# A decoder-layer kernel with a new column order, early x loads, joined RWKV output products and side work that waits for its tiling

## The chip, the cores and the metric

The kernel runs on one core of one Trainium2 chip. The metric is device microseconds (us) of one execution; lower is better. Its time before is the median of three runs.

## What is computed

One decoder layer with three token mixers beside each other (batch 1, 512 tokens, width 2048, float32), and a final norm:

```python
h = _rmsnorm(x, norm_w[l])
p = h @ w_in[l]                       # 2048 x 7824 columns
y_a = _rwkv7_mix(...)   # 16 heads of 64: generalized delta rule over 512 tokens
y_b = _moba_mix(...)    # 4 heads of 128: block-sparse causal attention
y_c = _gla_mix(...)     # 4 heads: gated linear attention with decay
mix = jnp.concatenate([y_a, y_b, y_c], axis=-1)
x = x + mix @ w_out[l]
return _rmsnorm(x, final_norm_w)
```

## The kernel before

**Projections.** Activations lie transposed: 16 tiles of 128 features by 512 tokens. Each tile of x is loaded (L1093), scaled by the norm weight into a part `hhi` (ScalarE, ACT) and a remainder `hlo` (VectorE, DVE). The division by the root mean square comes later, when a projected tile leaves its PSUM bank (`rstd_b`). A weight tile `raw` (128x512: four feature tiles of one 128-column job) is split in the same way into `hi` (ACT) and `lo` (DVE). A job of 128 columns is 16 feature tiles by three products of 128x512 (hhi·hi, hlo·hi, hhi·lo; helper `mmr`, L122), 48 in one of four PSUM banks `gb`. There are 61 such jobs and a narrow one (`low`). The string `ORDER` gives their order: `k0` is the first 128 columns of RWKV's k, `ga` its gate, `gq`, `gk`, `gv`, `gg` belong to GLA, `mq` to `mg` to MoBA. The first three jobs run interleaved, as each x tile arrives.

**Start.** ACT squares each x tile into one of three buffers, and GpSimd (POOL) adds the squares up (15 adds, L1107). `stats` then sums them over the partitions with four small products (`consts,f`), takes the inverse root on POOL (L377), and transposes the result into `rstd_b`. POOL runs in order; between its fifth and its sixth add stands the copy of `sel` (L1232) from the constants.

**Side work.** Everything else is written as Python generators (`spawn`): RWKV in four groups `q` of four heads, GLA in two, MoBA in four. They use four more PSUM banks `sb` (`bank`). A planner (`Clock`) adds up an estimated time of each engine while the program is being written; after each projection product `pump` resumes each side whose estimated inputs are there, and `force` resumes one that somebody must have. So the estimates fix the order of instructions on every engine, and nothing is decided on the chip. Products of the side work go through `mm` (L118, fp32, which the trace counts twice for each product) and `tr` (L127, transposes). Many of them use a part of the array: 128x64, 64x64, 64x128 or 32x32, against 128x128 for projections and transposes.

**RWKV.** For each pair of heads `j` in a group, `pair_r`, `pair_k`, `pair_v` form the inputs; the A stage (`AW,BK`, 64x128) makes the matrices, `solve` inverts the triangular ones on DVE (a DMA of `Ld` to DRAM and back, one multiplication by `n2l`, then some 60 short `scr` operations), and `pair_v` of `j = 1` needs `xr` (ACT and DVE, L135) for two products with `sel`. `chain` then walks eight chunks of 64 tokens; in each it makes the new state with four products `VS,BKt`. For each pair of chunks `y_pair` makes the outputs in two banks:

```python
for j in range(2):
    for h in range(2):
        ... mm(ps[h][r, j], AW[hr, c, j, 1], Sn[c % 3][hr, j], start=True, stop=False)
    for h in range(2):
        ... mm(ps[h][r, j], ARB[:, c, j, h], VS[:, c, j, h], start=(c == 0), stop=True)
```

The output projection (64 units with 12 products each) and the final norm follow when all sides are done.

Of the kernel before, what the change touches and what calls it, by code (L numbers as in the profile page):

```python
# [19 lines left out]
NC = S // C  # L20
# [19 lines left out]
ORDER = """wdad k0 ga0 ga1 r0 k1 low v0 r1 v1 gk0 gq0 gv1 gv0 gg1 gg0 k3 k2 gk1 gq1 r2  # L40
r3 v2 ga2 gv2 gg2 v3 ga3 gv3 gg3 mq0 k4 k5 r4 v4 r5 mg0 ga4 mv0 mk0 v5 k7
k6 mk1 mq1 ga5 mv1 r6 r7 v7 v6 mg1 ga6 mk2 mv2 mq2 mq3 mv3 mg2 mk3 ga7 mg3"""
# [15 lines left out]
MARGIN, BACKLOG = 0.1, 3.5  # L58
# [5 lines left out]
class Clock:  # L64


    def __init__(self):
        self.t = {"pe": 0.0, "dve": 0.0, "act": 0.0, "pool": 0.0, "dma": 0.0}
        self.cur = None
        self.table = None  # L70

# [23 lines left out]
def tile_hybrid(ctx: ExitStack, tc: tile.TileContext, x, xT, wu, wlow, wout, par, cst, w2a2_d, aup_d, fw, out):  # L95
# [19 lines left out]
    def mm(o, l, r, start=True, stop=True):  # L115
        m, n = numel(l), numel(r)
        ck.add("pe", 2 * max(m / 1.2, 2 * n / 2.4) / 1000)
        nc.tensor.matmul(o, l, r, start=start, stop=stop)  # L118

    def mmr(o, l, r, start, stop):  # L120
        ck.add("pe", numel(r) / 2400)
        nc.tensor.matmul(o, l, r, start=start, stop=stop)  # L122

    def tr(o, i):
        ck.add("pe", 0.107)
        k = i.shape[0]
        nc.tensor.transpose(o, i, ident[:k, :k])  # L127
# [50 lines left out]
    def dma(o, i, eng=None, est=3.0):  # L178
        if ck.cur is not None:
            ck.cur.ready = max(ck.cur.ready, ck.cur.start + est, ck.cur.end + est)  # L180
        (eng or nc.gpsimd).dma_start(o, i)
# [99 lines left out]
    def mixed(k, u):  # L281
# [6 lines left out]
        else:  # L288
            dma(mixd[k], u, nc.sync)
# [20 lines left out]
    def pump():  # L310

        for s in list(sides):
# [5 lines left out]
    def force(flag, what):  # L318

        while not flag():  # L320
            ready = [s for s in sides if runnable(s)]
            if not ready:
# [9 lines left out]
    def bank(n=1):  # L332
# [47 lines left out]
    def stats():  # L380
        yield lambda: squares[0] == KT
        ck.cur.start = max(ck.cur.start, ck.t["pool"])
# [7 lines left out]
        yield from rsqrt(rst[:, 4:8], rst[:, 0:4], 1.0 / D, NORM_EPS)  # L390
        b = yield from bank()
# [44 lines left out]
    def pair_decay(pr, j):  # L436
# [8 lines left out]
        b = yield from bank()  # L445
        mmr(sbk[b], w2hi[:, 0:128], wd, True, False)
        mmr(sbk[b], w2lo, wd, False, True)
        act(s0, sbk[b], AF.Sigmoid, bias=col(P_W0, pr))
        release(b)
        b = yield from bank()  # L450
        mmr(sbk[b], w2hi[:, 128:256], ad, True, False)
        mmr(sbk[b], a2lo, ad, False, True)
        act(s2, sbk[b], AF.Sigmoid, bias=col(P_A0, pr))
        release(b)
# [48 lines left out]
    def pair_v(pr, j):  # L503
# [10 lines left out]
        b = yield from bank()  # L514
# [36 lines left out]
    def bk_transposes(q):  # L551
        for c in range(0, NC, 2):
            b = yield from bank()
# [8 lines left out]
    def key_norms(q, j):  # L562
# [9 lines left out]
        dma(Nd[2 * j:2 * j + 2], n2t, nc.sync)  # L572
# [4 lines left out]
        for bl in range(2):  # L577
            for h in range(2):
                l0 = 32 * bl + 16 * h
                dma(n2l[l0:l0 + 16], Nd[h:4:2].rearrange("j (c b i) -> b j c i", b=2, c=NC)[bl], nc.sync)  # L580
# [8 lines left out]
    def solve():  # L589

        dma(Ld, Lt, nc.sync)
        yield None
        for bl in range(2):
            for h in range(2):
                r0, l0 = 64 * h + 32 * bl, 32 * bl + 16 * h
                dma(Lm[l0:l0 + 16], Ld[r0:r0 + 32, :, :, 32 * bl:32 * bl + 32].rearrange("i j c t -> (j c) i t"),
                    nc.sync)
# [15 lines left out]
        dma(Xd, NR[0:32], nc.sync)  # L613
        dma(Td, Lm, nc.sync)
        yield None
        for h in range(2):
            dma(T11[64 * h:64 * h + 32], Xd[16 * h:16 * h + 16].rearrange("l t s -> t l s"), nc.sync)
        for bl in (1, 0):
            for h in range(2):
                r0, l0 = 64 * h + 32 * bl, 32 * bl + 16 * h  # L620
                dma(Ttf[r0:r0 + 32, :, 32 * bl:32 * bl + 32], Td[l0:l0 + 16].rearrange("l s t -> s l t"), nc.sync)
# [24 lines left out]
    def y_pair(q, cp):  # L646

        bs = yield from bank(2)
# [11 lines left out]
        flags[f"ymm{q}"] = cp + 1  # L660
        yield None
        yo = Yq[:, cp].rearrange("p (r h n) -> p r h n", r=2, h=2)
# [8 lines left out]
    def chain(q):  # L671
# [3 lines left out]
        for c in range(NC):  # L675
# [21 lines left out]
            yield None  # L697
            if c < NC - 1:
                b = yield from bank()
# [18 lines left out]
            if c % 2:  # L718
                spawn(f"y{q} {c // 2}", y_pair(q, c // 2))
# [3 lines left out]
    def group_norm(q):  # L723
# [14 lines left out]
        for j in range(2):  # L738
            pr = 2 * q + j
            b = yield from bank()  # L740
# [33 lines left out]
    def load_w2a2(pr):  # L774
        dma(w2a2, w2a2_d[:, 256 * pr:256 * pr + 256], nc.sync)
# [24 lines left out]
    def by_chunks(src, parts):  # L800

        b = yield from bank()
# [12 lines left out]
    def gla(g):  # L815
# [14 lines left out]
        dma(aup, aup_d[:, 128 * g:128 * g + 128], nc.sync)  # L830
        if g == 0:
            yield from evac("low", lowT, rows=32)
            dma(lowd, lowT, nc.sync)
        else:
            dma(lowT, lowd, nc.sync)
# [31 lines left out]
        b = yield from bank()  # L867
# [23 lines left out]
        for w in range(4):  # L891
            b = yield from bank()
# [5 lines left out]
            for e in range(2):  # L898
# [6 lines left out]
                if e == 0:  # L905
                    yield None
                    bo = yield from bank(2)
# [22 lines left out]
        for i in range(2):  # L930
# [3 lines left out]
            b = yield from bank()  # L934
# [9 lines left out]
    def moba(h):  # L944
# [5 lines left out]
        def window(w, p, pT):  # L950
# [3 lines left out]
            b = yield from bank()  # L954
# [13 lines left out]
            b = yield from bank()  # L968
# [5 lines left out]
            b = yield from bank()  # L974
# [14 lines left out]
        b = yield from bank()  # L989
# [64 lines left out]
    loaded, split_done = 0, 0  # L1054
    late_adds, squares_of = [], []
# [41 lines left out]
    def square(n, r):  # L1097
# [6 lines left out]
        while late_adds and (len(late_adds) > 2 or n == KT - 1):  # L1104
            m, e = late_adds.pop(0)
            ck.add("pool", 1.25, e + 0.2)
# [33 lines left out]
    def split(i):  # L1140
        kind, n = items[i]
        dep = load_end[i]
        if kind == "x":
# [3 lines left out]
                               dep=max(dep, ck.t["act"] + 0.2))  # L1147
            squares_of.append((n, r))
# [251 lines left out]
```

## Time and profile before

| | |
|---|---|
| median of 3 runs | 1059.04 us (1058.44 to 1060.01) |
| the profiled execution | 1058.42 us, of which the span of its instructions 1056.7 us |
| mean granted TensorE clock | 0.995 of full speed |
| TensorE (PE) busy | 1035.9 us, 98% of the span |
| DVE, ACT, POOL busy | 666.3, 442.9, 71.9 us (63%, 42%, 7%) |
| DMA | 111.35 MB, 104 GB/s of HBM over the span |

The share of busy time says which engine has the least slack; the waits say where it stood still, and the chain of work that ended last is followed back from the last instruction to what released each step. A line number in a row is the line of the helper, so tiles (`gb`, `sb`, `VS`, `xr`) tell which step it is; `sb<-Sn,AW` is the product of `Sn` and `AW` into a side bank.

### The profile page before, as it was taken

What the parts mean: (1) busy time and instruction counts of PE and PEld (TensorE: products, weight loads), DVE (VectorE), ACT (ScalarE), POOL (GpSimd) and SP (SyncE); (2) the same over time, 40 slices, a digit from 0 to 9 for tenths busy, and PEclk for the clock granted to TensorE, in tenths of its full rate; (3) what the DMA queues carried; (4) which work ended last, traced back from release to release, by engine and by line L of the source; (5) the groups of instructions that cost most, each with busy time, mean ns of one, the idle gap of its engine ahead of it and who ended that gap; (6) DMA issues with size and microseconds to landing.
All of it is one profiled execution on the core that took longest, in us unless ns stands there. A gap on an engine that the chain in (4) does not pass through costs nothing.

```text
span 1056.7 us, 16747 instructions
## 1 busy us (share of the span) xinstructions
PE 1035.9 (98%) x6376; PEld 819.5 (78%) x6376; DVE 666.3 (63%) x1346; ACT 442.9 (42%) x789; POOL 71.9 (7%) x73
## 2 busy tenths in 40 slices
PE   7799999999999999999999999999999999999996
PEld 6587888767788887778888777888877788888885
DVE  6646759656756785676788665666965665424343
ACT  6464543343464433235434423545322365323333
POOL 4500000000100000001000001000000010202020
PEclk9899999999999999999999999999999999999999
DMA  7332333422233342223334222333341265343534
GB/s 253 100 93 78 92 92 98 111 56 84 81 108 88 98 115 74 71 81 114 92 99 119 67 71 70 90 99 86 115 111 51 71 223 175 109 142 100 160 119 159
DMA packets 80112, 111.35 MB, mean 105 GB/s; under 512 B 28176, under 2 KB 29392, under 8 KB 79904
## 3 DMA queue, kind: packets, MB, share of 16 engines
q1 hardware_dynamic: 79888, 109.23, 35.4%
q8 instruction: 50, 0.82, 0.3%
q0 software_dynamic: 144, 1.05, 0.2%
q14 instruction: 30, 0.25, 0.1%
HBM read 98.36 MB, written 11.89 MB: 104 GB/s over the span
## 4 chain that ended last, share of the span: by engine, by line
PE 97%; ACT 1%; POOL 1%; issue 0%; DMA 0%; DVE 0%; SPq 0%; ACTq 0%; POOLq 0%
PE gb L122 74%; PE sb L118 11%; PE sb L122 9%; PE sb L127 2%; POOL f L1107 1%; DMA raw<-in_wu_dram 0%; ACT hhi L175 0%; ACT hi L175 0%; DVE lo L135 0%; ACT f L175 0%; ACT pbuf L175 0%; ACT ARB L175 0%; DVE VS L135 0%; ACTq L1396 0%; POOLq L1396 0%
## 5 line engine op out<-in xcount | busy, mean ns | idle before, releaser
L122 PE MATMUL gb<-hhi,hi 128*128 128x512 f32 x976 | 404.1, 414 | 5.8 <-ACT hi L175 5.8
L122 PE MATMUL gb<-hhi,lo 128*128 128x512 f32 x976 | 383.5, 393 | 0.5 <-DVE lo L135 0.5
L122 PE MATMUL gb<-hlo,hi 128*128 128x512 f32 x976 | 382.9, 392 | 0.0
L175 ACT ACTIVATE hi<-raw 128x512 fp32r<-128x512 f32 x296 | 186.1, 630 | 394.5 <-PE gb L122 290.9
L135 DVE TENSOR_TENSOR lo<-raw,hi 128x512 fp32r<-128x512 f32 x296 | 212.7, 722 | 216.7 <-ACT hi L175 209.9
L122 PEld LDWEIGHTS gb<-hhi,hi 128*128 128x128 f32 x976 | 184.3, 189 | 49.6 <-ACT hi L175 6.0
L122 PEld LDWEIGHTS gb<-hhi,lo 128*128 128x128 f32 x976 | 184.1, 189 | 41.4 <-DVE lo L135 1.1
L122 PEld LDWEIGHTS gb<-hlo,hi 128*128 128x128 f32 x976 | 184.7, 189 | 34.2 <-DVE hlo L141 1.0
L135 DVE TENSOR_TENSOR scr<-scr 64x30 f32<-64x30 f32 (+14 forms) x240 | 77.5, 323 | 7.1
L122 PE MATMUL gb<-hi,hhi 128*128 128x512 f32 x128 | 50.0, 391 | 0.0
L122 PE MATMUL gb<-hi,hlo 128*128 128x512 f32 x128 | 49.8, 389 | 0.0
L122 PE MATMUL gb<-lo,hhi 128*128 128x512 f32 x128 | 49.8, 389 | 0.0
L175 ACT ACT_TABLE_LOAD x34 | 43.6, 1283 | 1.0 <-DVE VS L155 0.4
L155 DVE COPY VS<-sb 64x128 f32<-64x128 f32 x64 | 18.5, 288 | 32.8 <-PE sb L118 31.7
L377 POOL TENSOR_TENSOR gn<-gn,mhalf 128x16 f32<-128x16 f32 (+1 forms) x5 | 13.0, 2602 | 309.0 <-DVE gn L151 309.0
L175 ACT ACTIVATE Lt<-sb 64x256 f32<-64x256 f32 (+1 forms) x64 | 19.3, 326 | 33.1 <-PE sb L118 30.5
L175 ACT ACTIVATE f<-sb 64x256 f32<-64x256 f32 (+3 forms) x52 | 17.3, 363 | 36.1 <-PE sb L127 19.6
L122 PE MATMUL sb<-lo,hhi 128*128 128x512 f32 x80 | 31.2, 390 | 0.0
L122 PE MATMUL sb<-hi,hhi 128*128 128x512 f32 x80 | 31.2, 389 | 0.0
L122 PE MATMUL sb<-hi,hlo 128*128 128x512 f32 x80 | 31.2, 389 | 0.0
L122 PE MATMUL sb<-late,hhi 128*128 128x512 f32 x96 | 30.2, 395 | 0.0
L122 PEld LDWEIGHTS gb<-lo,hhi 128*128 128x128 f32 x128 | 24.0, 188 | 5.0
(230 smaller groups left out, 1140.5 us busy)
## 6 DMA issues: line engine op xcount, KB each, us to landing
raw<-in_wu_dram SPq DMA_DIRECT2D x244, 256.0 KB
raw<-in_wout_dram SPq DMA_DIRECT2D x64, 256.0 KB
f<-in_x_dram SPq DMA_DIRECT2D x16, 256.0 KB
hlo<-mix SPq DMA_DIRECT2D x15, 256.0 KB
Ld<-Lt SPq DMA_DIRECT2D x4, 512.0 KB
mix<-ARB SPq DMA_DIRECT2D x8, 256.0 KB
mix<-f SPq DMA_DIRECT2D x7, 256.0 KB
AW<-in_xT_dram SPq DMA_DIRECT2D x6, 256.0 KB
```

The costliest lines, as they stand in the source:

```text
L118: nc.tensor.matmul(o, l, r, start=start, stop=stop)
L122: nc.tensor.matmul(o, l, r, start=start, stop=stop)
L127: nc.tensor.transpose(o, i, ident[:k, :k])
L135: nc.vector.tensor_tensor(o, a, b, op=op)
L155: nc.vector.tensor_copy(o, a)
L175: nc.scalar.activation(o, a, f, **kw)
L377: nc.gpsimd.tensor_tensor(r, v, mhalf[:, 0:n], op=ALU.pow)
L1107: nc.gpsimd.tensor_tensor(fb[0], fb[0], fb[1 + m % 3], op=ALU.add)
```

## The change

Six things change. (1) `ORDER` is another permutation of the same jobs. (2) The planner's estimates are others: products of one tiling are cheaper and a change of tiling costs extra, an add on POOL costs 1.63 instead of 1.25, DMAs queue behind each other, and `pump` goes twice over the sides. (3) `bank` takes the tiling of the products to come, and waits up to 4 planned us (`PATIENCE`) until the engine is in it, unless the step is forced. (4) The products of `y_pair` are in `y_products`; where three banks are free at an odd chunk, they directly follow the `VS,BKt` products of that chunk, all `VS,ARB` first and all `Sn,AW` behind. (5) The loads of x tiles 4 to 15 are issued before weight loads that have to wait for a buffer. (6) The copy of `sel` stands behind the inverse root. The helper `dma` issues on SP alone.

```diff
+        old, self.tiling = self.tiling, tiling
+        if old != tiling:
+            whole = (old in "rf") + (tiling in "rf")
+            cost += 0.1 + 0.1 * (whole == 1) - 0.1 * (old == "r" and tiling == "f")
+        return self.add("pe", cost)
...
-        for s in list(sides):
+        for s in 2 * list(sides):
...
-    def bank(n=1):
+    def bank(n=1, tiling=None, patience=PATIENCE):
+
+        if tiling is not None and ck.tiling != tiling:
+            limit = ck.t["pe"] + patience
+            yield lambda: ck.tiling == tiling or forcing[0] or ck.t["pe"] > limit
...
-        ck.cur.start = max(ck.cur.start, ck.t["pool"])
+        ck.cur.start = max(ck.cur.start, ck.t["pool"] + 2.0)
...
         yield from rsqrt(rst[:, 4:8], rst[:, 0:4], 1.0 / D, NORM_EPS)
+        ck.add("pool", 0.3)
+        nc.gpsimd.tensor_copy(sel, consts[:, K_BD:K_BD + 130])
...
+    def y_products(q, cp, bs):
+
         ps = [sbk[b][:, 0:128].rearrange("p (r n) -> p r n", r=2) for b in bs]
         cs = [(2 * cp, slice(0, 64)), (2 * cp + 1, slice(64, 128))]
+        for j in range(2):
+            for h in range(2):
+                for c, r in cs:
+
+                    mm(ps[h][r, j], ARB[:, c, j, h], VS[:, c, j, h], start=(j == 0), stop=(c == 0), skip=True)
         for j in range(2):
             for h in range(2):
                 hr = slice(64 * h, 64 * h + 64)
                 for c, r in cs:
                     if c:
-                        mm(ps[h][r, j], AW[hr, c, j, 1], Sn[c % 3][hr, j], start=True, stop=False)
-            for h in range(2):
-                for c, r in cs:
-                    mm(ps[h][r, j], ARB[:, c, j, h], VS[:, c, j, h], start=(c == 0), stop=True)
+                        mm(ps[h][r, j], AW[hr, c, j, 1], Sn[c % 3][hr, j], start=False, stop=True, skip=True)
...
+            yb = None
             if c < NC - 1:
-                b = yield from bank()
+                if c % 2 and len(free_banks) >= 3:
+                    b, *yb = yield from bank(3)
+                else:
+                    b = yield from bank()
...
                         mm(pw[r, j], BKt[:, c, j, r], VS[:, c, j, h])
+                if yb is not None:
+                    y_products(q, c // 2, yb)
...
+    x_items = [i for i, (kind, n) in enumerate(items) if kind == "x" and n >= 4]
+    rest = [i for i in range(len(items)) if i not in x_items]
+    load_order = rest[:7]
+    for i, ahead in zip(rest[7:], (1, 3, 2, 3, 3)):
+        load_order += x_items[:ahead] + [i]
+        x_items = x_items[ahead:]
...
-            nc.gpsimd.tensor_copy(sel, consts[:, K_BD:K_BD + 130])
```

Three places of the order of instructions. First PE, in the RWKV output of the first two chunks of group 0 (`Sn_131` is the state after chunk 0). Before:

```order
L122 MATMUL gb_161<-hhi_87,lo_107 128x512
L118 MATMUL sb_168<-Sn_131,AW 64x64
L118 MATMUL sb_165<-Sn_131,AW 64x64
L118 MATMUL sb_168<-VS,ARB 64x64 x2
L118 MATMUL sb_165<-VS,ARB 64x64 x2
L118 MATMUL sb_168<-Sn_131,AW 64x64
L118 MATMUL sb_165<-Sn_131,AW 64x64
L118 MATMUL sb_168<-VS,ARB 64x64 x2
L118 MATMUL sb_165<-VS,ARB 64x64 x2
L122 MATMUL gb_161<-hhi_89,hi_100 128x512
```

And after:

```order
L133 MATMUL gb_161<-hhi_67,lo_105 128x512
L129 MATMUL sb_167<-VS,BKt 64x64 x4
L129 MATMUL sb_166<-VS,ARB 64x64 x2
L129 MATMUL sb_165<-VS,ARB 64x64 x2
L129 MATMUL sb_166<-VS,ARB 64x64 x2
L129 MATMUL sb_165<-VS,ARB 64x64 x2
L129 MATMUL sb_166<-Sn_131,AW 64x64
L129 MATMUL sb_165<-Sn_131,AW 64x64
L129 MATMUL sb_166<-Sn_131,AW 64x64
L129 MATMUL sb_165<-Sn_131,AW 64x64
L133 MATMUL gb_161<-hhi_69,hi_101 128x512
```

Four groups that alternate between two tilings (`Sn,AW` uses 64 rows of the array, `VS,ARB` and `VS,BKt` 128, all 64 columns) have become one of twelve products and one of the `Sn` products, in the same stay as the state products. Before, those stood by themselves 17 rows ahead.

Second DVE, around the first use of the statistics (`gn` from `sb_165` is their sum, the TENSOR_SCALAR on `gn` precedes POOL's inverse root, `lo` are weight remainders). Before:

```order
L141 SCALAR_TENSOR_TENSOR hlo_96<-sgt_147,params,hhi_95 128x512
L135 TENSOR_TENSOR lo_106<-raw_98,hi_102 128x512
L135 TENSOR_TENSOR lo_107<-raw_99,hi_103 128x512
L155 COPY gn<-sb_165 128x4
L135 TENSOR_TENSOR lo_104<-raw_97,hi_100 128x512
L151 TENSOR_SCALAR gn<-gn 128x4
```

And after:

```order
L152 SCALAR_TENSOR_TENSOR hlo_96<-sgt_147,params,hhi_95 128x512
L146 TENSOR_TENSOR lo_106<-raw_98,hi_102 128x512
L146 TENSOR_TENSOR lo_107<-raw_99,hi_103 128x512
L146 TENSOR_TENSOR lo_104<-raw_97,hi_100 128x512
L166 COPY gn<-sb_165 128x4
L146 TENSOR_TENSOR lo_105<-raw_98,hi_101 128x512
L162 TENSOR_SCALAR gn<-gn 128x4
```

The statistics stand one weight tile later on DVE, in front of the scaling is now `lo_105`. On PE their small products moved from behind projection product 108 to behind product 120, and the transposes of the result from behind 120 to behind 132.

Third DVE, from the solve of group 0 to `xr` of its second pair (the `scr` rows are steps of the solve). Before:

```order
L135 TENSOR_TENSOR lo_104<-raw_97,hi_100 128x512
L135 TENSOR_TENSOR f_152<-gb_164,rstd_b 128x512
L141 SCALAR_TENSOR_TENSOR vT<-pbuf_138,params,vT 128x512
L135 TENSOR_TENSOR lo_105<-raw_98,hi_101 128x512
L135 TENSOR_TENSOR scr<-scr 64x198
...
L135 TENSOR_TENSOR scr<-scr 64x12x19
L141 SCALAR_TENSOR_TENSOR f_152<-f_152,f_149 128x512
L135 TENSOR_TENSOR lo_106<-raw_99,hi_102 128x512
L135 TENSOR_TENSOR xr_122<-s_144,xr_121 128x512
```

And after:

```order
L146 TENSOR_TENSOR lo_107<-raw_99,hi_103 128x512
L152 SCALAR_TENSOR_TENSOR vT<-pbuf_138,params,vT 128x512
L146 TENSOR_TENSOR scr<-scr 64x198
...
L146 TENSOR_TENSOR scr<-scr 64x12x19
L146 TENSOR_TENSOR lo_104<-raw_97,hi_100 128x512
L146 TENSOR_TENSOR xr_122<-s_144,xr_121 128x512
```

Two operations on `f_152` (the evacuation of a gate and its product) and two weight remainders have gone from this stretch of DVE. On PE, the projection products between the last A-stage product of a group and the product that needs this `xr` were 99, 153, 204 and 102 in groups 0 to 3; they are 75, 150, 105 and 195.

## Rows read from the trace of the kernel before

**Rows 1.** Waits of PE: who waited for whom, us in total, times, longest.

```profile
PE sb L118 <- POOL f L1107: 6.0, 1, 6.0
```

**Rows 2.** A stretch: length, busy us (instructions) of PE, PEld, DVE, ACT, POOL, PE clock, DMA share, GB/s.

```profile
27.00:48.00 21.00, 14.56 (x57) 11.12 (x57) 14.89 (x15) 9.51 (x17) 14.93 (x13) 0.84 0.30 93
```

**Rows 3.** The chain that ended last, in order of time: start us, us, what.

```profile
42.20 4.53 PE gb L122 x12
...
144.35 1.99 PE sb L118 x32
...
344.21 1.09 PE sb L118 x16
...
355.08 27.93 PE gb L122 x123
```

**Rows 4.** Timeline of PE: start us, us, engine, line, operation, tiles, form, count.

```profile
215.25 0.40 PE L122 MATMUL gb<-hhi,lo 128*128 128x512 f32 x1
215.58 0.45 PE L118 MATMUL sb<-VS,BKt 128*64 128x64 f32 x8
215.96 0.50 PE L122 MATMUL gb<-hhi,hi 128*128 128x512 f32 x1
216.30 0.40 PE L122 MATMUL gb<-hlo,hi 128*128 128x512 f32 x1
```

**Rows 5.** Timeline of PE, in a `y_pair`.

```profile
244.29 0.34 PE L118 MATMUL sb<-Sn,AW 64*64 64x64 f32 x8
244.56 0.45 PE L118 MATMUL sb<-VS,ARB 128*64 128x64 f32 x8
```

**Rows 6.** Timeline of PE, transposes of an A stage.

```profile
148.45 0.60 PE L127 MATMUL sb<-consts,BK 128*128 128x128 f32 x4
148.81 0.71 PE L122 MATMUL sb<-xr,sel 128*128 128x512 f32 x2
```

**Rows 7.** Timeline of PE, the products of the statistics and the transposes of the result.

```profile
40.34 1.86 PE L118 MATMUL sb<-consts,f 128*128 128x1 f32 x8 [5.98 <-POOL f L1107]
...
46.57 0.60 PE L127 MATMUL sb<-consts,gn 128*128 128x128 f32 x4
```

**Rows 8.** Timeline of POOL at the start, with the idle time before a row and its releaser.

```profile
8.06 8.19 POOL L1107 TENSOR_TENSOR f<-f,f 128x512 f32<-128x512 f32 x5 [6.15 <-ACT f L175]
23.73 0.29 POOL L1232 CAST sel<-consts 128x130 fp32r<-128x130 f32 x1 [7.49 <-DMA consts<-in_cst_dram]
...
43.17 1.03 POOL L377 TENSOR_TENSOR gn<-gn,mhalf 128x4 f32<-128x4 f32 x1 [2.89 <-DVE gn L151]
```

**Rows 9.** Timeline of DVE at the start.

```profile
15.01 1.78 DVE L135 TENSOR_TENSOR lo<-raw,hi 128x512 fp32r<-128x512 f32 x1
16.71 0.74 DVE L141 SCALAR_TENSOR_TENSOR hlo<-AW,params,hhi 128x512 fp32r<-128x512 f32 x1
17.38 1.40 DVE L141 SCALAR_TENSOR_TENSOR hlo<-BK,params,hhi 128x512 fp32r<-128x512 f32 x2
```

**Rows 10.** Groups of POOL's instructions: line, operation, count | busy us, mean ns | idle before.

```profile
L1309 POOL TENSOR_TENSOR VS<-VS,AW 128x512 f32<-128x512 f32 x3 | 3.9, 1300 | 0.0
```

**Rows 11.** Timeline of SP: a weight load when its buffer came free.

```profile
34.18 0.33 SPq L1093 DMA_DIRECT2D raw<-in_wu_dram  x1
```

**Rows 12.** Timeline of ACT: the split that waited for that load.

```profile
36.77 0.63 ACT L175 ACTIVATE hi<-raw 128x512 fp32r<-128x512 f32 x1 [0.31 <-DMA raw<-in_wu_dram]
```

**Rows 13.** Timeline of PE, group 0: the products with that `xr`.

```profile
170.68 0.62 PE L122 MATMUL sb<-xr,sel 128*128 128x512 f32 x2
```

**Rows 14.** Timeline of DVE, group 0: first operation of the solve, and `xr`.

```profile
155.30 1.22 DVE L135 TENSOR_TENSOR scr<-scr,n2l 64x1024 f32<-64x1024 f32 x1 [3.14 <-DMA scr<-Ld]
...
169.69 0.68 DVE L135 TENSOR_TENSOR xr<-s,xr 128x512 fp32r<-128x512 f32 x1
```

**Rows 15.** Timeline of DVE, group 1: `xr`, and eight steps of the solve.

```profile
381.77 0.68 DVE L135 TENSOR_TENSOR xr<-s,xr 128x512 fp32r<-128x512 f32 x1
...
383.58 2.42 DVE L135 TENSOR_TENSOR scr<-scr 64x150 f32<-64x150 f32 x8
```

More of the change, by code (lines that the diff above doesn't have):

```diff
@@ L70, in __init__, with pe @@
         self.table = None
+        self.tiling = "r"
+    def pe(self, cost, tiling):
+        old, self.tiling = self.tiling, tiling
[3 more added lines that the diff above has]
+        return self.add("pe", cost)
     def add(self, eng, cost, dep=0.0):
@@ L112, in numel, with mm @@
         return n
-    def mm(o, l, r, start=True, stop=True):
+    def mm(o, l, r, start=True, stop=True, skip=False):
         m, n = numel(l), numel(r)
-        ck.add("pe", 2 * max(m / 1.2, 2 * n / 2.4) / 1000)
-        nc.tensor.matmul(o, l, r, start=start, stop=stop)
+        rows, cols = (min(q for q in (32, 64, 128) if q >= v) for v in (l.shape[0], m))
+        if rows == cols == 128:
+            ck.pe(2 * max(0.105, n / 1200 + 0.0025), "f")
+        else:
+            ck.pe(2 * (n / 2400 + 0.0025), f"{rows}x{cols}")
+        nc.tensor.matmul(o, l, r, start=start, stop=stop, skip_group_check=skip)
     def mmr(o, l, r, start, stop):
-        ck.add("pe", numel(r) / 2400)
+        ck.pe(numel(r) / 2400 + 0.0135, "r")
         nc.tensor.matmul(o, l, r, start=start, stop=stop)
     def tr(o, i):
-        ck.add("pe", 0.107)
+        ck.pe(0.0925, "f")
         k = i.shape[0]
@@ L513, in pair_v @@
         yield None
-        b = yield from bank()
+        b = yield from bank(1, "f")
         for w in range(4):
@@ L552, in bk_transposes @@
         for c in range(0, NC, 2):
-            b = yield from bank()
+            b = yield from bank(1, "f")
             for i in range(4):
@@ L655, in y_pair @@
                     if c:
-                        mm(ps[h][r, j], AW[hr, c, j, 1], Sn[c % 3][hr, j], start=True, stop=False)
-            for h in range(2):
-                for c, r in cs:
-                    mm(ps[h][r, j], ARB[:, c, j, h], VS[:, c, j, h], start=(c == 0), stop=True)
+                        mm(ps[h][r, j], AW[hr, c, j, 1], Sn[c % 3][hr, j], start=False, stop=True, skip=True)
         flags[f"ymm{q}"] = cp + 1
+    def y_pair(q, cp, bs=None):
+        if bs is None:
+            bs = yield from bank(2)
+            y_products(q, cp, bs)
         yield None
+        ps = [sbk[b][:, 0:128].rearrange("p (r n) -> p r n", r=2) for b in bs]
         yo = Yq[:, cp].rearrange("p (r h n) -> p r h n", r=2, h=2)
@@ L739, in group_norm @@
             pr = 2 * q + j
-            b = yield from bank()
+            b = yield from bank(1, "f")
             for cp in range(4):
@@ L800, in by_chunks @@
     def by_chunks(src, parts):
-        b = yield from bank()
+        b = yield from bank(1, "f")
         for w in range(4):
@@ L891, in gla @@
         for w in range(4):
-            b = yield from bank()
+            b = yield from bank(1, "64x64")
             for e in range(2):
@@ L933, in gla @@
             yield flag(f"gg{h}")
-            b = yield from bank()
+            b = yield from bank(1, "f")
             for w in range(4):
@@ L967, in window @@
             yield None
-            b = yield from bank()
+            b = yield from bank(1, "f")
             for i in range(w + 1):
@@ L973, in window @@
             yield flag(f"mv{h}")
-            b = yield from bank()
+            b = yield from bank(1, "f")
             for i in range(w + 1):
@@ L988, in moba @@
         yield from evac(f"mv{h}", fb[2])
-        b = yield from bank()
+        b = yield from bank(1, "f")
         for w in range(4):
@@ L1054, in tile_hybrid @@
     loaded, split_done = 0, 0
+    x_items = [i for i, (kind, n) in enumerate(items) if kind == "x" and n >= 4]
[4 more added lines that the diff above has]
+        x_items = x_items[ahead:]
+    load_order += rest[len(load_order) - 12 + len(x_items):]
+    assert not x_items and sorted(load_order) == list(range(len(items)))
     late_adds, squares_of = [], []
@@ L1167, in advance @@
         while split_done <= last:
-            while loaded < len(items) and (slot_of.get(loaded, 0) < NRAW
-                                           or last_in_slot[slot_of.get(loaded, 0) - NRAW] < split_done):
-                load(loaded)
+            while loaded < len(items):
+                i = load_order[loaded]
+                if slot_of.get(i, 0) >= NRAW and last_in_slot[slot_of[i] - NRAW] >= split_done:
+                    break
+                load(i)
                 loaded += 1
```

68 lines of the change are left out of this document (34 added, 34 removed).

## The prediction

> **What bounds the kernel now.** The waits of PE come first. The longest, 6.0 us for POOL [rows 1], lies at the start; after 48 us there is none. The busy time by stretches shows the same: from 27 to 48 us PE works for 14.56 of 21 us, at a granted clock of 0.84 [rows 2]. The chain of work that ended last is the same list: it runs on PE nearly alone, in stretches like 123 products in 27.93 us, or 0.227 each [rows 3]. So PE sets the time, and three things can be gained or lost: PE time itself, the start, and new waits where there were none. About 861 of the 1,036 busy us are 3,792 such products, which the change keeps.
>
> **PE time: groups of small products.** The timeline shows what a group costs. The last projection product before it starts 0.33 us ahead of it instead of 0.23, four products (eight in the trace) take 0.38, and the first projection product behind it takes 0.34 [rows 4]. So entering costs 0.10 more and returning 0.11. What of the 0.38 is fixed follows from the A stage: 16 products (32 in the trace) of 128 columns take 1.99 and eight take 1.09 [rows 3], so eight more cost 0.90, 0.11 each or 0.056 for 64 columns, and 0.19 of the group is fixed. The 0.38 is then four times 0.056 and 0.15 fixed. In `y_pair`, four `Sn,AW` take 0.27 up to the `VS,ARB` behind them [rows 5]; those have the shape of `VS,BKt`, and 0.38.
>
> I counted the groups in the order of both kernels. Those with tiling 128x64 go from 88 to 61, with 64x64 from 77 to 63, together 41 fewer by 0.15: -6.15. Those with 64x128 go from 10 to 12, by 0.19: +0.4. Entries from projections go from 122 to 124 (+0.2), returns to them from 121 to 113 (-0.9). Steps straight from transposes into a tiling go from 8 to 1; I take 0.09 for each, as an entry: -0.6. The sum is **-7.1 us**. A check by the pair: before, four groups (0.27 + 0.38, twice) and 0.21 for the excursion make 1.51. Joined, eight `VS,ARB` at 0.056 and eight `Sn,AW`, for which I take 0.27 + 4 x 0.056 = 0.49, add 0.94 to a stay that the state products had anyway: -0.57, eleven times; the five others save less. That this is most of 7.1 fits. The bounds: -4.5, if the `Sn` products keep the pace of a short group and the merged groups of GLA give nothing; -8, if each removed change also gives back an entry.
>
> The waiting for a tiling (`PATIENCE`) also gathers transposes: full-array groups go from 87 to 61. I cost this at nothing. Four transposes take 0.36 us from the start of the first to the next product [rows 6], 0.09 each, and the projection product before them starts the usual 0.23 ahead, so an excursion to them has no price to save. Bounds: -1 to +0.5, since each extra tiled neighbour could cost one entry of 0.1.
>
> **The start.** Before, the statistics stop PE: their products begin at 40.34 after 5.98 us of idleness [rows 7], because POOL did only five adds by 16.25 and then stood 7.49 us for the constants that the copy of `sel` needs [rows 8]. The low clock costs as well: behind the wait twelve products take 4.53 us [rows 3] where 2.72 is usual, and the eight small ones 1.73 (40.34 to 42.07, where the next begins). So product 120 is done at 46.57, where the transposes begin [rows 7].
>
> In the changed order POOL runs on without `sel`, and the x tiles are asked for earlier. Then DVE sets the pace: a two-input operation of 128x512 takes a step of 1.70 us beside a POOL add (15.01 to 16.71) and 0.67 without (16.71 to 17.38) [rows 9]. From 8.3 us on DVE has 24 such operations ahead of the last x tile's products, 15 beside adds and 9 not: 15 x 1.70 + 9 x 0.67 = 31.5, so at 39.8. Product 120 follows about three units' products later, some 0.7 us, at 40.5, with PE in short pauses but never for six us. That is 6.1 us earlier. A part is lost again. The scaling of the statistics on DVE now stands behind `lo_105`, whose weight load goes out when `lo_106` frees its buffer at about 40.5. Such a load was issued at 34.18 [rows 11], and ACT had it at 36.77 [rows 12]: 2.6. With the split on ACT (0.63), on DVE (0.67), the scaling (0.16) and POOL's 1.03 [rows 8] the inverse root is there at 45.6. PE is at its transposes at 40.5 + 0.44 (four small products) + 12 x 0.227 = 43.7, and waits 1.9; I take 2.6 with the semaphore steps between five engines. So the start gives 6.1 - 2.6 = **-3.5 us**. Bounds: -7 without that wait and with x tiles that let POOL's fifteen adds end at 33; +2 if x arrives as late as before and the new wait comes on top.
>
> A rule speaks against this gain. The rows show a pair of one add and one DVE operation in 1.70 us; apart, an add takes 1.30 [rows 10] and the operation 0.67. So they overlap by 0.27. The Trainium skill (SBUF — State Buffer, "Who interferes with whom") says that a DVE instruction with two SBUF inputs and a GpSimd instruction that reads SBUF contend for a shared port pair, and that the second to issue is blocked for the whole of the first. That the two slow each other this trace shows; a full exclusion it does not, as 1.70 is under 1.97. By the rule fifteen pairs would take 4.1 us more, and the start would give +0.6 instead of -3.5.
>
> **New waits.** The new order of columns pulls work closer together. In group 0 the products with `xr` of the second pair stand 24.3 us behind the end of the A stage (144.35 + 1.99, then 170.68) [rows 3, 13], and DVE had `xr` at 169.69 + 0.68 = 170.37 [rows 14], 0.3 ahead: DVE, which begins the solve at 155.30 when `Ld` has come back by DMA and then runs without a pause, is on the edge already. After, DVE has four operations like `xr` fewer in the stretch, 0.68 each by that row and about 0.6 as they overlap, so 24.0 - 2.4 = 21.6 us. PE has 75 projection products instead of 99 and 16 transposes, 17.0 + 1.5, with four `sel` products and entries 0.8: 19.3. It will wait **2.3 us**. In group 1 `xr` came 37.2 us after the A stage (345.3, that is 344.21 + 1.09, to 381.77 + 0.68) [rows 3, 15]. The change puts eight more steps of the solve ahead of it (2.35 [rows 15]), two evacuations (0.7) and two operations fewer (-1.2): 39.0 us. PE has 150 x 0.227 + 20 x 0.09 + 0.8 = 36.6: **2.4 us**. In group 2 I get 26.4 against 26.6, in group 3 45.4 against 46.6: no wait. Together **+4.8**. Bounds: 0, if the trip of `Ld` through DRAM is 2.4 us shorter, to +9, if groups 2 and 3 and the group norms wait as well.
>
> **The sum.** -7.1 - 3.5 + 4.8 = -5.8. The profiled execution took 1058.42 us (1056.7 of span and 1.7 around it), so 1052.6; the median lies 0.62 above that execution, so **1053.2 us**.
>
> **Rivals.** *The waits do not come* (chance 0.12): DVE gets `xr` in time since its operations move with it. Then -10.6, 1048.4. For it speaks that the planner reckons with the same operations; against it, that in both groups the reckoning is with measured stretches.
> *The gains are small* (0.08): -4.5 in PE time, nothing at the start because x comes too late, +4.8 in waits: 1059.3, no change. That the change does not do what it says, in that waiting for a tiling gathers only transposes, belongs here.
> *Adds and DVE operations exclude each other* (0.04): where fifteen adds run back to back, each pair takes 1.30 + 0.67. Then -7.1 + 0.6 + 4.8 = -1.7, 1057.3. The pairs of before took 1.70, which leaves it little. This is the rule of the page cited above.
> *Slower: the clock at the start* (0.06). Before, products behind the long wait ran at a lower clock: twelve in 4.53 us, 0.38 each [rows 3]. A start that DVE paces has many short pauses of PE; if these hold it at the lower of its two levels, 1.2 GHz, products take twice 0.227 from 27 to 45 us, and 18 us of such work are worth 9 us less the pauses, 8.5. It decides from about 8 us on, where it eats the gain: -5.8 + 8.5 = +2.7, 1061.7. Against it: PE had stood 5.98 us at once before it was slow [rows 7], and no pause of the new start is near that.
>
> **How the numbers follow.** The forecast has 0.70. About 0.2%, or 2.1 us, is what a measurement of this kernel can tell from no change. The forecast's own bounds reach a bit into that, the first rival lies beyond: faster 0.80, same 0.14, slower 0.06. The range from 1047.5 to 1057.5 takes in the forecast with its bounds and most of the first rival, and leaves out most of the others.
>
> **What would show it.** Right: no wait of PE for the adds of POOL, product 120 near 40.5 us, a wait of 2 to 3 us before the transposes of the statistics; PE waits for DVE `xr` twice, near 163 and 378 us; groups of twelve products `VS,BKt` and `VS,ARB` of about 0.84 us; PE busy 7 us less. Wrong: idle PE after 48 us of over 8 us, a clock under 0.9 from 27 to 45 us, or PE busy unchanged.

## The result

The changed kernel takes **1054.49 us** (median of 5 runs, 1052.84 to 1055.10) against 1059.04 (1058.44 to 1060.01): a ratio of 0.9949, 95% interval 0.9937 to 0.9962. Forecast were 1053.2 and a range of 1047.5 to 1057.5. The profiled execution took 1054.49 us, of which the span is 1052.6, 4.1 less than before.

The page of the changed kernel, its span and busy time (PE is 6.3 us less busy than in the table of before; busy time counts slow products too, before the change at the start and here behind a wait told of below, so 6.3 is not yet the work saved):

```profile
span 1052.6 us, 16723 instructions
PE 1029.6 (98%) x6376; PEld 814.9 (77%) x6376; DVE 669.7 (64%) x1346; ACT 441.9 (42%) x790; POOL 74.8 (7%) x73
```

The waits of PE in the changed kernel (who waited for whom: us in total, times, longest):

```profile
PE gb L133 <- ACT hi L186: 5.8, 1, 5.8
PE sb L133 <- DVE xr L146: 4.0, 2, 2.4
PE gb L133 <- DVE hlo L152: 1.8, 4, 0.7
PE sb L138 <- POOL gn L398: 1.4, 1, 1.4
PE sb L138 <- DVE Lt L146: 0.9, 1, 0.9
```

The 6.0 us for POOL's adds [rows 1] are gone. In their place stand four short pauses for `hlo`, 1.4 us for the statistics, and, where there was no wait, 4.0 us for `xr` and 0.9 for `Lt`.

**The start.** POOL in the changed kernel, with idle time and releaser in brackets; it answers to [rows 8]:

```profile
8.07 11.58 POOL L1150 TENSOR_TENSOR f<-f,f 128x512 f32<-128x512 f32 x7 [6.16 <-ACT f L186]
21.55 6.76 POOL L1150 TENSOR_TENSOR f<-f,f 128x512 f32<-128x512 f32 x4 [1.91 <-ACT f L186]
29.49 5.20 POOL L1150 TENSOR_TENSOR f<-f,f 128x512 f32<-128x512 f32 x3 [1.17 <-ACT f L186]
35.78 1.28 POOL L1150 TENSOR_TENSOR f<-f,f 128x512 f32<-128x512 f32 x1 [1.09 <-ACT f L186]
43.13 1.03 POOL L398 TENSOR_TENSOR gn<-gn,mhalf 128x4 f32<-128x4 f32 x1 [6.06 <-DVE gn L162]
```

The adds end at 37.06 instead of 40.3, and PE at the statistics, to be held beside [rows 7], has 120 projection products done when it comes to them and 132 at the transposes:

```profile
37.67 0.50 PE L133 MATMUL gb<-hlo,hi 128*128 128x512 f32 x1 [0.25 <-DVE hlo L152]
...
38.95 0.95 PE L129 MATMUL sb<-consts,f 128*128 128x1 f32 x8
...
44.22 0.65 PE L138 MATMUL sb<-consts,gn 128*128 128x128 f32 x4 [1.45 <-POOL gn L398]
44.62 0.48 PE L133 MATMUL gb<-hhi,hi 128*128 128x512 f32 x1
```

Before, the transposes at 46.57 had 120 products ahead of them. Twelve more at 0.227 would have been 2.7 us later, at about 49.3; the changed kernel is there at 44.2, so it leads by 5.1 us.

**PE work.** A joined group in the changed kernel (timeline of PE; the count is twice that of the program):

```profile
222.22 0.45 PE L129 MATMUL sb<-VS,BKt 128*64 128x64 f32 x8
222.50 0.64 PE L129 MATMUL sb<-VS,ARB 128*64 128x64 f32 x16
223.07 0.46 PE L129 MATMUL sb<-Sn,AW 64*64 64x64 f32 x16
223.46 0.50 PE L133 MATMUL gb<-hhi,hi 128*128 128x512 f32 x1
```

Twelve products take 0.85 us up to the `Sn` group, and the eight `Sn,AW` 0.39.

**What came back.** The stretches around the second wait for `xr` (columns as in [rows 2]), and the chain behind it:

```profile
376.00:379.00 3.00, 0.61 (x3) 0.20 (x2) 2.76 (x10) 0.63 (x1) 0.00 (x0) 0.98 0.43 132
379.00:382.00 3.00, 3.00 (x8) 2.33 (x9) 2.76 (x8) 0.29 (x1) 0.64 (x2) 0.50 0.31 87
382.00:385.00 3.00, 3.00 (x14) 2.41 (x13) 2.51 (x4) 0.49 (x2) 0.00 (x0) 0.95 0.17 54
```

```profile
378.07 0.69 DVE xr L146
...
379.54 8.90 PE gb L133 x33
```

PE stood 2.39 us, and then the granted clock was at the lower of its two levels, 1.2 GHz: 33 products took 8.90 us instead of 33 x 0.227 = 7.49. That wait cost 2.4 and 1.4.

So the difference of 4.1 us divides as follows: 5.1 gained until the statistics are done; 5.1 lost in waits behind 48 us (4.0 and 0.9 of the list, and 0.2 for `VS`); 1.4 in slow products behind one of them; and what remains, 4.1 - 5.1 + 5.1 + 1.4 = 5.5, is less PE work. Counted directly it is 5.5 too: PE's busy time from the 150th projection product to the end (columns as in [rows 2]) is 994.48 us before and 990.38 in the changed kernel, of which 1.4 are the slow products.

```profile
53.64:1060.00 1006.36, 994.48 (x6216) 786.86 (x6214) 630.40 (x1305) 411.74 (x737) 44.65 (x43) 1.00 0.35 101
48.59:1060.00 1011.41, 990.38 (x6216) 784.92 (x6214) 631.09 (x1306) 412.07 (x739) 47.08 (x43) 0.99 0.34 101
```

### The profile page after: what moved, and what is told of

It reads as the page before. It is cut to its first block, busy times and chain, and to the rows that moved or that the text cites. A ratio compares the mean times of both kernels' runs of the same rounds, so it can differ in the third digit from the quotient of the medians.

```text
span 1052.6 us, 16723 instructions
## 1 busy us (share of the span) xinstructions
PE 1029.6 (98%) x6376; PEld 814.9 (77%) x6376; DVE 669.7 (64%) x1346; ACT 441.9 (42%) x790; POOL 74.8 (7%) x73
## 4 chain that ended last, share of the span: by engine, by line
PE 89%; DVE 5%; issue 2%; DMA 2%; ACT 1%; SPq 0%; POOL 0%; ACTq 0%; POOLq 0%; DVEq 0%
PE gb L133 67%; PE sb L129 10%; PE sb L133 9%; PE sb L138 2%; DVE scr L146 2%; DVE lo L146 2%; DMA raw<-in_wu_dram 1%; DVE hlo L152 1%; DMA scr<-Ld 0%; DMA Ld<-Lt 0%; DMA AW<-in_xT_dram 0%; ACT hhi L186 0%; DVE gn L170 0%; DVE Lt L146 0%; ACT hi L186 0%
## 5 line engine op out<-in xcount | busy, mean ns | idle before, releaser
L133 PE MATMUL gb<-hhi,hi 128*128 128x512 f32 x976 | 399.9, 410 | 5.8 <-ACT hi L186 5.8
```

## The experiments

Each median stands beside runs of the kernel before on the same chip, whose median was 1059.02 to 1059.44 throughout. Two kernels whose intervals overlap are not told apart by their medians; what is said of them then rests on the traces, each of which is one execution.

| kernel | median us | ratio to before (95%) |
|---|---|---|
| before + copy of `sel` moved | 1055.42 | 0.9968 (0.9956 to 0.9980) |
| before + x ahead | 1058.23 | 0.9994 (0.9985 to 1.0002) |
| before + both | 1053.20 | 0.9945 (0.9933 to 0.9958) |
| changed, `sel` back | 1056.22 | 0.9976 (0.9967 to 0.9985) |
| changed, statistics' scaling behind their copy | 1052.52 | 0.9943 (0.9930 to 0.9955) |
| changed, `xr` early | 1051.68 | 0.9937 (0.9925 to 0.9950) |
| changed, these two repairs | 1052.14 | 0.9934 (0.9922 to 0.9946) |
| changed, alternating groups | 1060.98 | 1.0018 (1.0009 to 1.0028) |
| changed, no waiting for a tiling | 1059.58 | 1.0004 (0.9995 to 1.0013) |
| changed, old column order | 1072.09 | 1.0130 (1.0114 to 1.0146) |
| before + both + grouped `y_pair` | **1049.67** | 0.9910 (0.9897 to 0.9924) |
| changed, once more | 1053.62 | 0.9946 (0.9934 to 0.9959) |

### The start: which of its parts

Only the copy moved, in the kernel before:

```diff
         yield from rsqrt(rst[:, 4:8], rst[:, 0:4], 1.0 / D, NORM_EPS)
+        nc.gpsimd.tensor_copy(sel, consts[:, K_BD:K_BD + 130])
...
-            nc.gpsimd.tensor_copy(sel, consts[:, K_BD:K_BD + 130])
```

> The kernel before with one line moved: the copy of sel stands behind the inverse root on POOL instead of between its fifth and sixth add. Loads, column order and PE order stay as before. Theory A (the copy in POOL's queue is what stopped PE for 6 us): the wait of PE for the adds shrinks to under 2 us, the clock stays up from 27 to 48 us, and the time falls by 4 to 6 us, to 1053 to 1055. Rival (late x tiles hold the adds in any case): the wait stays at 5 us or more and the time is within 1 us of 1059.

It took 1055.42 us, just outside theory A's figure, and the wait shrank as it said. The waits, and the stretch of [rows 2] in that kernel:

```profile
PE sb L118 <- POOL f L1108: 1.9, 1, 1.9
```

```profile
27.00:48.00 21.00, 18.79 (x74) 14.90 (x73) 16.07 (x18) 8.24 (x14) 11.27 (x12) 0.84 0.41 128
```

In one point theory A was wrong: PE is 4.2 us busier in this stretch than in [rows 2], but the clock is at 0.84 still, behind a wait of 1.9 us. The profiled execution was also the slowest of six (1057.65, mean clock 0.995); the two with a mean clock of 0.998 took 1053.63 and 1054.08. So the copy in POOL's queue was what held PE; but the low clock of before did not need six idle us.

Only the loads, by the change's `load_order`, in the kernel before:

> The kernel before with the x tiles 4 to 15 loaded ahead of blocked weight loads, sel still copied between the adds. Theory A: POOL still stands until the constants have landed, at 23 to 25 us, and does ten adds after it, so PE waits 4 us or more for them and the time stays within 2 us of 1059. Rival (late x): the adds end by 36 us, and the time falls by 4 us or more.

1058.23 us, and PE waited 3.7 us for the adds, a little under what theory A asked; they end at 40.98, since POOL stands for the constants as before. The loads alone are worth some 0.8 us, which the interval does not tell from nothing.

Both together:

> The kernel before with both changes of the start that leave PE's order alone: sel copied behind the inverse root, and the x tiles loaded ahead. The statistics keep their place behind projection product 108. If the two add up, 3.6 and 0.8 us, the time is 1054 to 1055. If the later place of the statistics on PE (behind product 120) is what pays once the adds are early, this gives no more than the moved copy alone, 1055 to 1056, with 1.5 to 2 us of waits at the statistics.

1053.20 us, 5.9 less than its before, where 3.6 and 0.8 add up to 4.4; the intervals are too wide to call that more than the sum. The same stretch, and PE and DVE at the statistics:

```profile
27.00:48.00 21.00, 19.58 (x90) 15.53 (x90) 16.84 (x18) 10.19 (x18) 11.53 (x12) 1.00 0.34 102
```

```profile
37.66 0.95 PE L118 MATMUL sb<-consts,f 128*128 128x1 f32 x8
...
41.62 0.65 PE L127 MATMUL sb<-consts,gn 128*128 128x128 f32 x4 [0.81 <-POOL gn L377]
```

```profile
40.10 0.15 DVE L155 COPY gn<-sb 128x4 f32<-128x4 f32 x1
40.28 0.17 DVE L151 TENSOR_SCALAR gn<-gn 128x4 f32<-128x4 f32 x1
```

With both, PE has 90 matmuls in the stretch against 74, and the clock stays up. But the loads did not leave the order alone, though the expectation says so. By the count in the trace the planner put the statistics behind product 114 and the transposes behind 123, and on DVE the scaling came directly behind the copy; the kernel with the loads alone has the same two places on PE. Behind product 108, done at 35.4, the statistics would have waited about 1.1 us for the adds, which end at 36.49 here (an estimate from the trace). So whether their later place is needed for the gain has not been separated. The main finding does not hang on it: **these two edits alone are as fast as the whole change**, 1053.20 us against 1054.49 and 1053.62, with overlapping intervals.

The copy put back into the changed kernel:

> The changed kernel with the copy of sel back at its old place, all else as changed (statistics behind projection product 120, x tiles ahead). If the moved copy by itself carries the gain at the start, POOL's adds end near 40 us again and the time rises by 4 to 5 us, to 1058 to 1059. If the later place of the statistics on PE carries it, PE has twelve products to do in that time, waits about 1 us more at most, and the time stays within 1.5 us of 1054.5.

1056.22 us, 1.7 more, and PE waited only 0.4 us for the adds: by the time this lies near the second case. By the start it lies nearer the first. POOL's ten adds behind the copy, PE at the transposes, and the stretch of [rows 2] in that kernel:

```profile
24.94 16.36 POOL L1148 TENSOR_TENSOR f<-f,f 128x512 f32<-128x512 f32 x10
```

```profile
47.17 0.65 PE L138 MATMUL sb<-consts,gn 128*128 128x128 f32 x4 [0.32 <-POOL gn L398]
```

```profile
27.00:48.00 21.00, 17.47 (x68) 12.07 (x67) 15.83 (x16) 10.96 (x19) 15.54 (x13) 0.92 0.29 87
```

The adds end at 41.30, and the transposes stand at 47.17 instead of 44.22: the copy costs 2.95 us of the 5.1 that the start had gained. Some 2 us of them come back later, because here the second wait for `xr` is 1.8 us and no slow products follow it. So the later place of the statistics keeps about 2.1 us of the gain, and the place of `sel` gives the rest.

The scaling directly behind the copy of the statistics, in the changed kernel:

```diff
         vcopy(rst[:, 4:8], sbk[b][:, 0:4])
         release(b)
-        yield None
         yield from rsqrt(rst[:, 4:8], rst[:, 0:4], 1.0 / D, NORM_EPS)
```

> The changed kernel with one pause of the planner taken out, so that on DVE the scaling of the statistics follows directly on their copy instead of behind a weight remainder that waits for its load. Theory (the 1.4 us wait before the transposes of the statistics is DVE's order): the wait goes, and the time falls by 1.5 to 2 us, to 1052.5 to 1053. Rival (POOL or the planner's other work delays it as much): the wait stays at 1 us or more and the time within 0.7 us of 1054.5.

1052.52 us, 2.0 less by the median, with overlapping intervals. The trace shows that no wait is left at the transposes, which now begin at 42.37 behind product 129: 1.2 us earlier than in the changed kernel when the three products are allowed for. DVE in that kernel:

```profile
40.38 0.16 DVE L166 COPY gn<-sb 128x4 f32<-128x4 f32 x1
40.58 0.17 DVE L162 TENSOR_SCALAR gn<-gn 128x4 f32<-128x4 f32 x1
42.49 0.69 DVE L146 TENSOR_TENSOR lo<-raw,hi 128x512 fp32r<-128x512 f32 x1 [1.75 <-ACT hi L186]
```

In the changed kernel the scaling had stood behind such a `lo`, at 42.89. The theory holds for the wait and its cause; that it is worth 1.5 to 2 us is more than the trace shows.

### The PE work: groups of small products

Every instruction at its place, only the products within a `y` in the order of before (the lines that tell the planner the old sum are left out):

```diff
         for j in range(2):
             for h in range(2):
-                for c, r in cs:
-                    mm(ps[h][r, j], ARB[:, c, j, h], VS[:, c, j, h], start=(j == 0), stop=(c == 0), skip=True)
...
-        for j in range(2):
-            for h in range(2):
                 hr = slice(64 * h, 64 * h + 64)
                 for c, r in cs:
                     if c:
-                        mm(ps[h][r, j], AW[hr, c, j, 1], Sn[c % 3][hr, j], start=False, stop=True, skip=True)
+                        nc.tensor.matmul(ps[h][r, j], AW[hr, c, j, 1], Sn[c % 3][hr, j], start=True, stop=False)
+            for h in range(2):
+                for c, r in cs:
+                    nc.tensor.matmul(ps[h][r, j], ARB[:, c, j, h], VS[:, c, j, h], start=(c == 0), stop=True)
```

> The changed kernel with every instruction at its place, but within each stay of the RWKV output the Sn and ARB products alternate between the two tilings as before (Sn, ARB, Sn, ARB). 44 more groups of 128x64 and 64x64. Theory (each group has a fixed cost of 0.15 us on PE): PE busy rises by 5 to 7 us, waits stay as they are, and the time rises to 1060 to 1061. Rival (the fixed part is hidden in the weight loads once groups follow each other directly): within 1.5 us of 1054.5.

```profile
PE 1035.4 (98%) x6376; PEld 818.2 (77%) x6376; DVE 669.8 (63%) x1346; ACT 442.5 (42%) x790; POOL 75.0 (7%) x73
```

1060.98 us, and PE 5.8 us busier: 0.13 for each of the 44 groups. But the wait for `xr` was shorter here (3.1 in all, longest 1.7) and the clock did not fall, so the changed kernel's 1.4 us of slow products hide a part. Without them, and without the start, the price comes out clearer. PE from the 150th projection product to the end (columns as in [rows 2]), in the changed kernel once more, whose clock did not fall either (its run is told of further below), and in this one:

```profile
49.45:1060.00 1010.55, 988.70 (x6216) 783.82 (x6214) 630.96 (x1306) 411.71 (x739) 47.09 (x43) 1.00 0.35 101
48.69:1060.00 1011.31, 995.42 (x6216) 787.54 (x6214) 631.14 (x1306) 412.38 (x739) 47.14 (x43) 1.00 0.34 101
```

That is 6.7 us more, or 0.15 for each group, 27 of 128x64 and 17 of 64x64. The theory holds. This grouping is the whole of the change's PE gain: with these groups back, PE works no shorter than in the kernel before (994.48 us in the same stretch).

No waiting for a tiling (the test in `bank` replaced by `if False`):

> The changed kernel with bank never waiting for a tiling; the planner then places some side work otherwise, with 81 full-array groups instead of 61 and 65 of 64x64 instead of 63. Theory (an excursion to transposes has no fixed price): PE busy without its waits rises by no more than 1 us, and what the time changes beyond that is in waits that the trace lists. Rival (each gathered excursion saves 0.2 us): PE busy without waits rises by 4 us, to a time of 1058 to 1059.

```profile
PE 1031.8 (98%) x6376; PEld 814.6 (77%) x6376; DVE 668.6 (63%) x1346; ACT 435.4 (41%) x785; POOL 74.7 (7%) x73
```

```profile
PE sb L133 <- DVE xr L146: 5.3, 4, 2.5
```

1059.58 us, 5.1 more than the changed kernel: by the time the rival's figure, by its cause neither. The waits for `xr` are four instead of two, and 5.3 us. PE busy rose by 2.2, more than the theory allowed and less than the rival asked. Transposes themselves cost as before (four in 0.35 to 0.36 us in both), so no price of an excursion appears; but I cannot assign the 2.2. So about half of what patience is worth here is that it leads the planner to a placement with fewer waits, which is not a price one could carry elsewhere, and the cause of the other half stays open.

### The waits for xr

`xr` of the second pair made before the evacuation of that pair's `v`, so that DVE does not have it behind the solve:

```diff
     def pair_v(pr, j):
+        if j == 1:
+            yield from parts(s3[j])
         yield from evac(f"v{pr}", pbuf[j][:, 1:S + 1])
         yield from shift_mix(pbuf[j], 16 + pr, vT)
-        yield from parts(s3[j])
+        if j == 0:
+            yield from parts(s3[j])
```

> The changed kernel with the split of xr for the second pair of each group made before the evacuation of that pair's v, so that it does not stand behind steps of the solve in DVE's order. Theory (the two waits of PE for xr, 4.0 us, and the slow products behind the longer one, some 1.4 us, are a cost of the new column order that hides 5 us of its gain): both waits go, the clock stays at full speed near 380 us, and the time falls by 4 to 6 us, to 1049 to 1050.5. Rival (DVE is behind in that stretch in any case, and the next step waits instead): waits of the same sum appear at bv, at the transposes of vT or in the chain, and the time stays within 1.5 us of 1054.5.

```profile
PE sb L129 <- DMA BK<-Xd: 2.2, 4, 1.4
```

```profile
379.00:382.00 3.00, 3.00 (x16) 2.47 (x16) 2.79 (x6) 1.11 (x3) 0.64 (x2) 1.00 0.27 87
```

1051.68 us, 2.8 less than the changed kernel by the median, with overlapping intervals. In the trace both waits for `xr` and the one for `Lt` are gone, and the clock stays up near 380 us. (The planner also placed other side work anew, so this is not the one split alone.) But 2.2 us of waits came at the next step of the solve, for its DMA (`Xd`): half of the rival is right too, though not with the steps that it named. 4.9 and 1.4 less 2.2 would be 4.1; the profiled execution (1050.59, the fastest of five) gained 3.9.

With the statistics' repair as well:

> The changed kernel with both repairs: xr of the second pair split early, and the scaling of the statistics directly behind their copy. If the two waits are independent, the gains add: 1051.7 less 1.5 to 2, so 1049.7 to 1050.2. If an earlier start only moves the first wait for the solve, it stays at 1051 to 1052.

1052.14 us, no better than one of them alone within what five runs tell (1049.44 to 1053.86). Its waits for `Xd` are 2.1 us, the longest 1.6. The median lies near the second outcome. The profiled execution, the fastest of the five, has neither wait and gained 5.1 us, against 1.7 and 3.9 in the profiles of the two alone; the other four had a lower mean clock (0.994 to 0.995 against 0.998), and where they lost it no trace shows. So whether the gains add stays open.

The old column order in the changed kernel:

> The changed kernel with the column order of before, all else as changed; the planner places the side work anew. Theory (the two waits for xr come from the new column order): the waits of PE for xr shrink to under 1.5 us in all. The groups stay as few (60 of 128x64, 65 of 64x64), so PE busy stays within 3 us of 1029.6. What else the time does is then other waits of PE that the old order has under the new rules; I expect one or two, and a time above 1054.5. Rival (the waits come from the planner's new costs): xr waits of 3 us or more stay.

```profile
PE gb L135 <- DVE f L148: 12.0, 2, 6.6
PE gb L135 <- DVE pbuf L148: 3.9, 1, 3.9
PE sb L135 <- DVE xr L148: 0.3, 1, 0.3
```

1072.09 us. As the theory says, the wait for `xr` falls to 0.3. For group 0 that is clean: between 48 us and there PE waits for nothing, `xr` ends at 159.89 and its products begin at 159.99. By group 1 PE had already stood 7.8 us for other things, which gave DVE time, so there it is not shown that the order alone does it. And 16 us of other waits appear, where PE finds no free bank until DVE has evacuated one (`f`, `pbuf`). PE busy rose by 4.2, more than I allowed; the clock was at the lower level behind each of the three long waits, and by the count of slow products some 2.6 of the 4.2 are that. So under the planner's new rules the new order is the better one. The new order under the old rules was not run, so what each is worth alone is not known.

### Put together, with as little moved as possible

The two edits of the start, and in `y_pair` all `ARB` products before all `Sn`, with the planner told the old sum, so that against the kernel with the start alone not one other instruction moves:

> The kernel before with both changes of the start (sel moved, x ahead), and within each y_pair all ARB products first and all Sn products behind, every instruction otherwise at its place: 16 groups of 128x64 and 9 of 64x64 fewer, the planner's sums as before, so no step moves. Theory (a group has a fixed price of 0.15 us, and the waits for xr came from the new placement, not from fewer groups): 25 x 0.15 = 3.8 us less PE work than e2b_x_sel and no new wait, so 1049 to 1050. Rival (each gain of PE time brings DVE's xr onto the path, since it was only 0.3 us ahead before): the saving lies behind the products with xr in each RWKV group, so it costs at most where it precedes them; then 1051 to 1053, with waits for xr in the trace.

```profile
span 1048.1 us, 16748 instructions
PE 1030.1 (98%) x6376; PEld 814.3 (78%) x6376; DVE 669.4 (64%) x1346; ACT 442.5 (42%) x789; POOL 71.9 (7%) x73
```

```profile
PE sb L118 <- POOL f L1124: 0.6, 1, 0.6
PE sb L127 <- POOL gn L377: 0.5, 1, 0.5
```

**1049.67 us**, faster than both kernels. PE busy 1030.1 is 3.5 less than the 1033.6 of the kernel with the start alone, 0.14 for each of 25 groups. From the 150th projection product on it is 4.1, or 0.16 each; first the kernel with the start alone, then this one:

```profile
48.03:1060.00 1011.97, 994.73 (x6216) 787.11 (x6214) 630.45 (x1305) 411.68 (x737) 44.60 (x43) 1.00 0.35 101
48.89:1060.00 1011.11, 990.66 (x6216) 784.83 (x6214) 630.53 (x1305) 411.60 (x737) 44.63 (x43) 1.00 0.35 101
```

There is no wait for `xr`. The theory holds in both halves.

The changed kernel, unaltered, beside it on the same chip:

> The changed kernel itself, unaltered, beside the run above on the same chip: 1054.5 within 1 us.

1053.62 us, 4.0 above the one just told of, with intervals that lie apart.

## Why the prediction was right, and where its terms were off

The forecast case came: faster, by a gain at the start and in PE work less new waits for `xr`. Term by term:

- **The start: -3.5 forecast, -5.1 measured.** The mechanism was right, down to the scaling behind `lo_105` (at 42.89) and the pause before the transposes. The term was mis-sized at both ends. I had product 120 follow the last of 24 DVE operations, done at 39.8, and end at 40.5. The pairs came nearly as I reckoned: POOL stood 1.9, 1.2 and 1.1 us for squares, and still fourteen of the fifteen adds fell beside a DVE operation of 1.70 us. But PE's last wait for DVE, at 37.67, was for the last `hlo` but one, and product 120 was done 1.3 us behind it, at 38.95. And I put 2.6 us for the new wait, of which 0.7 was an allowance without a row; it was 1.45.
- **PE work: -7.1 forecast, about -5.5 measured.** The twelve joined products were right (0.85 for 0.84) and the `Sn` group was cheaper than my check had it (0.39 for 0.49). The price of a group held: 0.15 to 0.16 on the average of both tilings, so 41 fewer are the 6.15 forecast, and with the 0.4 for 64x128 that leaves 5.75. What failed is the rest of the sum, -1.3 for entries, returns and steps from transposes into a tiling. With the 44 groups put back, the changed kernel has all other such savings still, and PE works 0.9 us more than before (995.42 and 994.48), about what its three more groups of 64x64 and two of 64x128 cost. So they gave nothing; why a saved return is worth nothing, no run shows.
- **New waits: +4.8 forecast (the two waits add up to 4.7); 4.0 measured where I forecast them, 0.9 and 0.2 beside.** The first `xr` wait was 1.62 us at 161.9 (forecast 2.3 near 163), the second 2.39 at 378.8 (2.4 near 378). The 0.9 for `Lt` and the 0.2 for `VS` stand in no term. That DVE was on the edge before, by 0.3 us, was the reading that decided this term.
- **Missed:** the 1.4 us of slow products behind the second wait. I had asked what a low clock would do at the start, and not what it would do behind a wait that I forecast myself.
- **The rule of the Trainium skill** (SBUF — State Buffer, "Who interferes with whom") did not bring the time that it would give. Pairs of 1.30 + 0.67 would have left the start without a gain, and it gained 5.1; the pairs took 1.65 to 1.70 us as before, not 1.97 (seven adds in 11.58 us are 1.65 each).
- **The rivals.** "The waits do not come" fell by the trace. "Slower: the clock at the start" did not come in the changed kernel, but it was no idle thought: in the kernel with the copy of `sel` moved alone, the clock was low at the start behind a wait of only 1.9 us, and in the changed kernel with the copy back it was at 0.92 though no pause of PE from 27 us to the statistics was over 0.8 us. My reason against it, that PE had stood six us before it was slow and no pause of the new start is near that, did not carry.

That 1053.2 came so near 1054.49 is in part luck: the start gave 1.6 us more than its term and PE work 1.6 less, and these cancel; what is left is mostly the missed 1.4. In the result, too, much cancelled: 5.5 us of PE work against 6.5 us of waits and their slow products. The gain of the start alone is as large as the result.

## What to carry to other kernels

Before moving work closer together, look for the operation that is ready only just in time (here 0.3 us on DVE, in the order behind a long solve): taking work out from in front of the product that needs it makes it a wait, while 4 us less PE work elsewhere did not. Take the gains that move little first, such as order within a group and a copy out of a queue; here they gave 9.8 us, where the larger change gave 4.5 to 5.8. Look in the trace, too, at what an edit moved that was meant to move nothing, as the loads did here with the statistics. And cost a wait of TensorE with the products behind it, not only with its own length.

## What the runs showed of the hardware that I had not expected

Whether a wait lowers the clock differs between executions of one kernel. In the changed kernel the wait for `xr` of 2.4 us was followed by a stretch at 0.50; in the same kernel run once more a wait of 2.3 us at the same place was not:

```profile
376.00:379.00 3.00, 1.27 (x6) 0.71 (x4) 2.76 (x11) 0.63 (x1) 0.00 (x0) 1.00 0.68 175
379.00:382.00 3.00, 2.40 (x10) 1.99 (x11) 2.79 (x8) 0.63 (x1) 0.64 (x2) 1.00 0.20 55
```

Of ten executions of the changed kernel, six had a mean clock of 0.996 (1054.37 to 1055.10 us) and four 0.998 (1052.64 to 1053.62). The means of the two lie 1.7 us apart, near the 1.4 us of slow products; that it is this wait in the executions that were not traced is likely, and not shown.
